# A planner's duration table for operations on few partitions, and the order of work at the beginning and at the entry of the MLP

## The chip, the cores and the metric

The kernel runs on one core of one Trainium2 chip. The metric is the device time of one execution in microseconds (us); the times of a kernel are told as the median of several executions. The engines are named as the profile names them: PE is TensorE's matmul, PEld its weight load, DVE is VectorE, ACT is ScalarE, POOL is GpSimd, SP is SyncE, whose queue issues most of the DMAs. [...]

## The reference

One layer of a decoder trunk in float32, with 1024 positions and a width of 1024, and 256 memory tokens:

```python
h = rms_norm(x, norm_mix)
p = h @ w_in                       # columns: RWKV r,k,v,w,a,g | conv B,C,x | gate A | gate B
p_rw = p_rw + (token_shift(p_rw) - p_rw) * mu_shift
out_a = rwkv7_branch(r, k, v, wd, ad, gd, ...)   # recurrence over 1024 positions, 8 heads of 64
out_b = short_conv_branch(cb, cc, cx, conv_w)    # B * conv3(C * x)
merged = sigmoid(ga + bg_a) * (out_a @ w_proj_a) + sigmoid(gb + bg_b) * (out_b @ w_proj_b)
x = x + merged @ w_out_mix
x = x + memory_cross_attention(rms_norm(x, norm_xattn), rms_norm(mem, norm_mem), ...)
hm = rms_norm(x, norm_mlp)
x = x + square(relu(hm @ w_up)) @ w_down         # 4096 hidden columns
return rms_norm(x, norm_final)
```

## The kernel before

All activations are held transposed: 128 columns of the width on the partitions, positions along the free axis, in two blocks of 512 positions. Every large matrix product is exact to float32 by splitting both factors into a high and a low part ("hi", "lo", type fp32r) and adding three matmuls of 128x128 by 128x512: hi by hi, hi by lo, lo by hi. A weight tile is loaded into a raw buffer (names `wr`), its hi half is made by ACT (`wh`) and its lo half by DVE (`wl`); a `+` behind such a name (`wr+`, `wh+`) marks a tile that lies in the large pool of 44 buffers called H, where the activations (`H`, `P`) live too.

**A planner sets the order.** The program is written as generators ("streams"): the main stream walks through the stages below, and side streams load weights, split them, make the constants, and do the recurrence. A `Scheduler` (lines 40 to 235) runs them in one pass when the program is built. Each instruction goes through `Proxy.call` (line 253, the line that nearly all rows of the profile show), which books it in `note` on a clock of its engine: it starts when its engine is free and its operands are written, and lasts what `cost` (line 68) says for ACT, DVE and POOL, and what `pe` (line 91) says for PE. `shared` (line 186) lengthens DVE's and POOL's operations on SBUF where they overlap. A stream that yields `need(tile)` (line 199) is called again once PE's planned clock has passed the planned end of the tile's writing by 0.7 us. So the table in `cost` does not change what is computed; it decides how many matmuls of the main stream are put on PE between two steps of a side stream, and which operation stands ahead of which on the in-order queues of DVE, ACT, POOL and SP. On the chip the engines wait for each other by semaphores; the planned clock is not there.

**The stages.** (1) The beginning: `x_stage` (line 997) transposes the two blocks of x on PE, each in two halves of four column groups; ACT and DVE take the transposes out of PSUM as hi and lo (`H`) with the gain applied, while the first pair of column tiles of the projection is accumulated in PSUM tiles psg and psy. `x_scale` (line 985) squares the block's rows on ACT, and gives the factor 1/rms, which PE transposes over the partitions (psg<-ident,sm) into `Rt`; the factor is applied when a tile is taken out. `constants` (line 686) transposes a table of gains (`vrow`, rows from DRAM in a tile st) on PE. (2) The projection, `gemm` over the list `PROJ` (line 584): 46 column tiles x 2 blocks, 24 matmuls for each block of a tile. `proj_evac` (line 1123) takes each out. Between these matmuls stand the steps of the recurrence as side streams: `wkv_prepares` (factors of a window of positions), `wkv_inverts` (products of 64x128 operands into pss, taken out by DVE on 64 partitions, and an inverse), `wkv_chains` (the state, 64x64 products in psc). There are eight windows. (3) `mem_k` and `mem_v` (lines 1623, 1640) make keys and values of the memory tokens with half-wide weights ("light" weights), then `merge` (line 1701) the two gated branches. (4) A residual product, the attention, a second residual product (h3). (5) The MLP: `up_products` (line 857) computes 16 pairs of tiles with seven products in place of eight (a Strassen-like scheme; `PRODUCTS`, line 842, gives for each its number p, PSUM tile, weight and half). A product is 4 operands k x 3 matmuls. Products 1 and 2 take the plain halves of the activations, products 6, 5, 7, 3 sums of them; `up_operands` (line 895) makes the sums on POOL and the hi and lo parts on ACT and DVE. The weights of a pair come as a "quad" of two raw buffers; `w_split_quad` (line 466) makes four weight tiles of it: the plain one (ACT, DVE), then four POOL operations, then three more. `w_splits` (line 509) does this quad after quad. (6) `mlp_down`, the same way.

The numbers behind a tile's name (psg_2075) count allocations. A tag has few buffers (3 of psg, 2 of pss, 2 of psc, 1 of psy; the raw buffers `wr` are 2 and some of H), so an instruction also waits for the reader of the buffer's last content.

Of the kernel before, what the change touches and what calls it, by code (L numbers as in the profile page):

```python
# [10 lines left out]
F32R = mybir.dt.float32r  # L11
# [30 lines left out]
class Scheduler:  # L42
# [25 lines left out]
    def cost(self, eng, meth, aps):  # L68
        n = self.size(aps[0])
        psum = any(self.key(a).startswith("ps") for a in aps)  # L70
        if eng == "ACT":
            return (0.05 if psum else 0.093) + (0.093 if len(aps) > 2 else 0.0) + n / 1200
        if eng == "DVE":
            if meth == "reciprocal":
                return 0.07 + n * 0.0066
            if meth == "tensor_reduce":
                n = self.size(aps[1])
# [181 lines left out]
def tile_hybrid_block(  # L259
# [147 lines left out]
    def w_raw(i):  # L407
        n = 2 if i in quads else 1
        more = i >= first_quad and (i - first_quad) % 2 if i in quads else i > first_quad and i % 4 > 1
# [15 lines left out]
    def w_loads():  # L425
        for i in range(2, len(wlist)):
            if i < first_quad:
                yield lambda: i < ws["split"] + 2
# [37 lines left out]
    def w_split_quad(raws):  # L466
# [15 lines left out]
        yield room_  # L482
        hi, lo = tiles()
        yield from halves(hi[:], lo[:], ra)
        w_made(hi, lo)
        yield need(lo)
# [22 lines left out]
    def w_splits():  # L509
        for i in range(2, len(wlist)):  # L510
            yield lambda: i < ws["raw"]
            raw = ws["raws"].pop(i)
            if i in quads:
                yield need(*raw) - 0.2
                yield from w_split_quad(raw)
                ws["split"] += 1
                ws["live"] -= 2
                continue
# [167 lines left out]
    def constants():  # L686
        yield until(("h", 0, 3))
        yield need(vrow) + 1.0
        vps = ps("y", [P, P])
# [167 lines left out]
    def up_products(ops, hook):  # L857
# [3 lines left out]
        for i in range(NP_):  # L861
            banks, wt, tmp = {}, [], {}
            if i == NP_ - 1:
                done.add(("up", "last"))
            for p, tag, w, half in PRODUCTS:
# [29 lines left out]
    def up_operands(raw, ops):  # L895


        t2 = {}
# [8 lines left out]

        yield until(("o", 1, 7))
        lh["n"] = 32
        for k in range(4):  # L910
# [4 lines left out]
            yield until(("h3", 0, 2 * k))  # L915
            a = raw[k][0]
            yield from make(1, k, a[:, 0], ("h3", 0, 2 * k))
            yield until(("h3", 0, 2 * k + 1))
            b = raw[k][1]
            yield from make(2, k, b[:, 0], ("h3", 0, 2 * k + 1))  # L920
            yield until(("h3", 1, 2 * k), ("h3", 1, 2 * k + 1))
# [63 lines left out]
    def x_scale(b, xs, ss):  # L985
        cs = slice(0 if b else TB, D)
        for i in range(4):
            ACT.activation(xs[i][:, cs], xs[i][:, cs], AF.Square, accum_out=ss[:, 4 + i:5 + i])
# [8 lines left out]
    def x_stage(b, tags):  # L997
# [7 lines left out]
        for h in range(2):  # L1005
# [8 lines left out]
            for k in range(4):  # L1014
# [11 lines left out]
                done.add(("h", b, n))  # L1026
        done.add(("x", b))
# [102 lines left out]
    def proj_stream(t, b, o):  # L1130
# [59 lines left out]
        elif kind == "cx":  # L1190
            if (i, b) == (3, 1):
                drop(1)
# [959 lines left out]
```

## Time and profile before

| | |
|---|---|
| time, median of 3 runs (lowest to highest) | 1808.51 us (1805.92 to 1813.68) |
| the profiled execution | 1810.48 us, of which its span 1808.8 us |
| mean granted clock of TensorE | 0.991 |
| busy: PE / PEld / DVE / ACT / POOL | 1745.7 / 1423.7 / 1078.6 / 696.6 / 524.4 us |
| moved by DMA | 289.19 MB |

The profile is one execution. A row of the timeline gives the start, the duration, the engine, the operation with out<-in, and how many like it follow one another; the bracket behind it holds the time the engine stood idle before it and what released it. A matmul's duration includes its passage through the array, and matmuls overlap: a 128x512 one reads 0.39 us, while the next one starts 0.23 us later. PE is busy for 97% of the span, so the views that matter are those of the other 63 us: what PE waited for, and where its clock was not granted in full.

### The profile page before, as it was taken

Reading aid. Unit: us, or ns where it says so; the run is one execution under the profiler, and the core shown is the slowest. Engines: PE = TensorE matmul, PEld = TensorE weight load, DVE = VectorE, ACT = ScalarE, POOL = GpSimd, SP = SyncE. Lnnn points to the kernel's source line nnn. Section 1 sums busy time; section 2 is a strip of 40 time slices with the busy share of each in tenths; the row PEclk is TensorE's granted clock in tenths of the full one; section 3 lists DMA queues with packets and bytes.
Section 4 is the critical chain, followed back from the end, with each engine's and each line's share of the span. In section 5 each row is a group of like instructions: output and inputs, shape, how many; then the busy total and the mean of one; then the engine's idle time right before and its main releaser. Section 6 shows DMA issues by size and latency. Waiting matters only on the chain.

```text
span 1808.8 us, 26674 instructions
## 1 busy us (share of the span) xinstructions
PE 1745.7 (97%) x9914; PEld 1423.7 (79%) x9914; DVE 1078.6 (60%) x1694; ACT 696.6 (39%) x1233; POOL 524.4 (29%) x872
## 2 busy tenths in 40 slices
PE   7899999999999999999999999999999999999998
PEld 5687777877767778988888877778888888888887
DVE  4478675665664443555546665577677776655543
ACT  4624333132234433422333334354444444534532
POOL 2117653664465110001323344342232310000000
PEclk9999999999999999999999999999999999999999
DMA  6543532423435436645745667334544469765431
GB/s 211 204 118 104 164 103 56 117 74 103 111 94 159 139 95 209 208 140 190 233 152 187 192 185 263 105 111 158 182 149 165 151 219 350 259 208 196 152 123 52
DMA packets 303360, 289.19 MB, mean 160 GB/s; under 512 B 40745, under 2 KB 223135, under 8 KB 303231
## 3 DMA queue, kind: packets, MB, share of 16 engines
q1 hardware_dynamic: 302158, 286.97, 49.7%
q8 instruction: 78, 1.28, 0.3%
q10 hardware_dynamic: 1072, 0.53, 0.1%
q14 instruction: 52, 0.42, 0.1%
HBM read 193.06 MB, written 94.37 MB: 159 GB/s over the span
## 4 chain that ended last, share of the span: by engine, by line
PE 75%; DVE 8%; DMA 5%; POOL 4%; issue 3%; ACT 3%; SPq 1%; ACTq 0%; POOLq 0%; DVEq 0%
PE psg L253 50%; PE pss L253 12%; PE psc L253 9%; DVE P L253 4%; PE psy L253 4%; POOL ex L253 3%; ACT P L253 2%; SPq L253 1%; DVE wl L253 1%; DMA sh<-d_ob 1%; DVE st L253 1%; POOL P L253 1%; DVE sh L253 1%; ACT st L253 1%; DMA P<-dn 1%
## 5 line engine op out<-in xcount | busy, mean ns | idle before, releaser
L253 PE MATMUL psg<-H,wh 128*128 128x512 f32 x1808 | 583.6, 400 | 2.6 <-ACT H L253 1.4
L253 PEld LDWEIGHTS psg<-H,wh 128*128 128x128 f32 x1808 | 338.1, 190 | 73.9 <-ACT H L253 2.3
L253 PE MATMUL psg<-P,wh 128*128 128x512 f32 (+1 forms) x1240 | 371.2, 380 | 6.6 <-ACT P L253 3.0
L253 PE MATMUL psg<-H,wl 128*128 128x512 f32 x888 | 355.2, 400 | 0.0
L253 PEld LDWEIGHTS psg<-P,wh 128*128 128x128 f32 x1240 | 227.9, 188 | 50.6 <-ACT P L253 3.4
L253 PE MATMUL psg<-P,wl 128*128 128x512 f32 (+1 forms) x620 | 235.6, 380 | 0.0
L253 ACT ACTIVATE wh<-wr 128x1024 fp32r<-128x1024 f32 (+2 forms) x187 | 137.8, 764 | 229.5 <-PE psg L253 126.2
L253 DVE TENSOR_TENSOR wl<-wr,wh 128x1024 fp32r<-128x1024 f32 (+2 forms) x178 | 161.2, 928 | 83.3 <-ACT wh L253 77.7
L253 PEld LDWEIGHTS psg<-H,wl 128*128 128x128 f32 x888 | 168.7, 190 | 34.3
L253 ACT ACTIVATE P<-P 128x512 fp32r<-128x512 f32 (+3 forms) x246 | 147.8, 635 | 78.5 <-DVE P L253 41.9
L253 DVE TENSOR_TENSOR P<-P,P 128x512 fp32r<-128x512 f32 (+2 forms) x204 | 150.2, 773 | 19.1 <-ACT P L253 17.8
L253 POOL TENSOR_TENSOR sm<-sm,mhalf 128x8 f32<-128x8 f32 (+2 forms) x18 | 23.7, 1317 | 427.6 <-DVE sm L253 427.6
L253 PEld LDWEIGHTS psg<-P,wl 128*128 128x128 f32 x620 | 116.8, 188 | 21.8 <-DVE wl L253 0.6
L253 POOL TENSOR_TENSOR ex<-ex,P 128x60 f32<-128x60 f32 (+24 forms) x248 | 97.4, 393 | 102.9 <-DMA P<-dn 88.1
L253 POOL TENSOR_TENSOR ex<-ex 128x60 f32<-128x60 f32 (+24 forms) x248 | 100.4, 405 | 19.4
L253 PE MATMUL pss<-P,wh 128*128 128x512 f32 x296 | 91.7, 390 | 1.1 <-DVE P L253 1.1
L253 ACT ACTIVATE P<-psc,sm 64x64 f32<-64x64 f32 (+1 forms) x128 | 42.4, 332 | 105.4 <-PE psc L253 62.3
L253 DVE TENSOR_SCALAR P<-psc,sm 64x64 f32<-64x64 f32 x120 | 34.9, 291 | 77.9 <-ACT P L253 72.6
L253 PE MATMUL psc<-P,P 128*64 128x64 f32 (+2 forms) x816 | 66.5, 247 | 12.9 <-DVE P L253 10.0
L253 DVE TENSOR_TENSOR P<-psg,P 128x512 f32<-128x512 f32 x44 | 30.3, 689 | 80.8 <-PE psg L253 67.5
L253 PEld LDWEIGHTS psc<-P,P 128*64 128x64 f32 (+2 forms) x816 | 45.2, 143 | 38.6 <-issue 17.2
L253 PE MATMUL psc<-P,wh 128*128 128x512 f32 x216 | 67.4, 393 | 0.0
(686 smaller groups left out, 2812.9 us busy)
## 6 DMA issues: line engine op xcount, KB each, us to landing
P<-d_t SPq DMA_DIRECT2D x56, 512.0 KB
wr<-in_w_in_dram SPq DMA_DIRECT2D x40, 512.0 KB
d_t<-P SPq DMA_DIRECT2D x64, 256.0 KB
d_x<-P SPq DMA_DIRECT2D x48, 256.0 KB
P<-d_x SPq DMA_DIRECT2D x24, 512.0 KB
d_t<-st SPq DMA_DIRECT2D x48, 256.0 KB
d_tg<-st SPq DMA_DIRECT2D x32, 256.0 KB
wr<-in_w_kv_dram SPq DMA_DIRECT2D x16, 512.0 KB
```

The source lines that it names most:

```text
L253: return fn(*args, **kw)
```

## The change

Seven edits, without a change to what is computed. (1) In `cost`, operations on fewer than 128 partitions get durations of their own: ACT 0.1 us more above 64 elements a partition; DVE 0.17 us (0.2 for scalar_tensor_tensor) with 0.08 more from 5 to 64 elements; and reciprocal and tensor_reduce on DVE get 0.11 and 0.12 us more. (2) The light weights use raw buffers in H as well, and after the projection are loaded up to four ahead; the tiles of `merge` are allocated one at a time. (3) Of the first two quads the plain weight tile is made first, of both, and then the rest of both. (4) `constants` waits 6 us rather than 1 us after the table's landing as planned, and transposes it in psg, not psy. (5) `up_products` takes products 1 and 2 of pairs 0 and 1, then the rest of pair 0, the rest of pair 1, and the others as before; the operands of products 1 and 2 are made by a stream of their own, ahead. (6) For the second block of x the squares are written to a spare tile and their stream is started between its two halves rather than after them. (7) Two waits keep the parts of a short-convolution tile in their order.

```diff
--- before.py
+++ after.py
@@ -67,14 +67,17 @@
         n = self.size(aps[0])
+        part = aps[0].shape[0] < 128
         psum = any(self.key(a).startswith("ps") for a in aps)
         if eng == "ACT":
-            return (0.05 if psum else 0.093) + (0.093 if len(aps) > 2 else 0.0) + n / 1200
+            return (0.05 if psum else 0.093) + (0.093 if len(aps) > 2 else 0.0) + n / 1200 + (0.1 if part and n > 64 else 0.0)
         if eng == "DVE":
             if meth == "reciprocal":
-                return 0.07 + n * 0.0066
+                return 0.18 + n * 0.0066
             if meth == "tensor_reduce":
-                n = self.size(aps[1])
+                return 0.19 + self.size(aps[1]) * 0.00104
+            if part:
+                return (0.2 if meth == "scalar_tensor_tensor" else 0.17) + (0.08 if 4 < n <= 64 else 0.0) + n * 0.00104
             if meth in ("tensor_scalar", "tensor_copy") and not psum:
@@ -406,7 +409,7 @@
         n = 2 if i in quads else 1
-        more = i >= first_quad and (i - first_quad) % 2 if i in quads else i > first_quad and i % 4 > 1
+        more = i >= first_quad and (i - first_quad) % 2 if i in quads else (i > first_quad or i in light) and i % 4 > 1
         raw = ws["raws"][i] = [sb("wr+" if more else "wr", wlist[i][1]) for _ in range(n)]
@@ -425,7 +428,7 @@
             if i < first_quad:
-                yield lambda: i < ws["split"] + 2
+                yield lambda: i < ws["split"] + (4 if i in light and "proj" in done else 2)
             else:
@@ -463,7 +466,7 @@
         ws["made"] += 1
-    def w_split_quad(raws):
+    def w_split_quad(raws, first=True, rest=True):
         n = KD // 2
@@ -479,11 +482,14 @@
         room_ = lambda: ws["made"] < ws["closed"] + 3
-        yield room_
-        hi, lo = tiles()
-        yield from halves(hi[:], lo[:], ra)
-        w_made(hi, lo)
-        yield need(lo)
+        if first:
+            yield room_
+            hi, lo = tiles()
+            yield from halves(hi[:], lo[:], ra)
+            w_made(hi, lo)
+        if not rest:
+            return
+        yield need(raws[0], raws[1])
         s2 = sb("st", [P, n, P])
@@ -511,10 +517,21 @@
                 yield need(*raw) - 0.2
-                yield from w_split_quad(raw)
-                ws["split"] += 1
-                ws["live"] -= 2
+                if i == first_quad:
+                    yield from w_split_quad(raw, rest=False)
+                    before = raw
+                elif i == first_quad + 1:
+                    yield from w_split_quad(raw, rest=False)
+                    for r in (before, raw):
+                        yield from w_split_quad(r, first=False)
+                        ws["split"] += 1
+                        ws["live"] -= 2
+                else:
+                    yield from w_split_quad(raw)
+                    ws["split"] += 1
+                    ws["live"] -= 2
                 continue
@@ -685,8 +702,8 @@
         yield until(("h", 0, 3))
-        yield need(vrow) + 1.0
-        vps = ps("y", [P, P])
+        yield need(vrow) + 6.0
+        vps = ps("g", [P, P])
         yield need(vps)
@@ -858,11 +875,14 @@
-        for i in range(NP_):
-            banks, wt, tmp = {}, [], {}
+        all_ = [({}, [], {}) for _ in range(NP_)]
+        order = [(i, PRODUCTS[:2]) for i in range(2)] + [(i, PRODUCTS[2:]) for i in range(2)] + \
+            [(i, PRODUCTS) for i in range(2, NP_)]
+        for i, products in order:
+            banks, wt, tmp = all_[i]
             if i == NP_ - 1:
                 done.add(("up", "last"))
-            for p, tag, w, half in PRODUCTS:
+            for p, tag, w, half in products:
                 if w == len(wt):
@@ -895,6 +915,7 @@
@@ -905,20 +926,22 @@
             done.add(("up", p, k))
+        def plain():
+            for k in range(4):
+                for e in range(2):
+                    yield until(("h3", 0, 2 * k + e))
+                    yield from make(1 + e, k, raw[k][e][:, 0])
         lh["n"] = 32
+        sch.spawn(plain(), first=True)
         for k in range(4):
             t2[k] = tt[:, k % 2]
-            yield until(("h3", 0, 2 * k))
-            a = raw[k][0]
-            yield from make(1, k, a[:, 0], ("h3", 0, 2 * k))
-            yield until(("h3", 0, 2 * k + 1))
-            b = raw[k][1]
-            yield from make(2, k, b[:, 0], ("h3", 0, 2 * k + 1))
-            yield until(("h3", 1, 2 * k), ("h3", 1, 2 * k + 1))
+            yield until(("up", 1, k), ("up", 2, k), ("h3", 1, 2 * k), ("h3", 1, 2 * k + 1))
+            a, b = raw[k]
             yield need(a, b)
@@ -984,8 +1007,9 @@
         cs = slice(0 if b else TB, D)
+        junk = sb("P", [P, D]) if b else None
         for i in range(4):
-            ACT.activation(xs[i][:, cs], xs[i][:, cs], AF.Square, accum_out=ss[:, 4 + i:5 + i])
+            ACT.activation(junk[:] if b else xs[i][:, cs], xs[i][:, cs], AF.Square, accum_out=ss[:, 4 + i:5 + i])
         yield need(ss)
@@ -1024,8 +1048,9 @@
                 done.add(("h", b, n))
+            if h == (1, 0)[b]:
+                sch.spawn(x_scale(b, xs, ss))
         done.add(("x", b))
-        sch.spawn(x_scale(b, xs, ss))
         for k in range(KD):
@@ -1190,6 +1215,7 @@
                 drop(1)
+            yield until(("cc", i, b))
             u = sb("sh", [P, TB + 2])
@@ -1209,7 +1235,9 @@
             prevs["cy", i, b] = y
+            done.add(("cy", i, b))
         elif kind == "cb":
+            yield until(("cy", i, b))
             z = sb("st", [P, TB])
@@ -1702,6 +1730,8 @@
         wh, wl = w_[0]
+        for t in (mgh, mgl):
+            t.append(two(sb("H", [P, S], F32R)))
         for b in range(NB):
@@ -2094,8 +2124,7 @@
         done.add("proj")
-        mgh = [two(sb("H", [P, S], F32R)) for _ in range(KD)]
-        mgl = [two(sb("H", [P, S], F32R)) for _ in range(KD)]
+        mgh, mgl = [], []
         for k, n in MIX:
```

Edits (1) and (6) move other work than their own lines. On ACT at the beginning, before (P_98 to P_104 are the rows of the second block, H_164 to H_167 the hi parts of its second half's columns, st_482 an operand of the decay's small product):

```order
L253 ACTIVATE P_184<-psg_390 128x512
L253 ACTIVATE H_164<-pss_398,gmix 128x512
L253 ACTIVATE st_482<-sh_445,omu 128x512
L253 ACTIVATE st_487<-sh_448,omu 128x512
L253 ACTIVATE H_165<-pss_399,gmix 128x512
L253 ACTIVATE P_181<-pss_399 128x512
L253 ACTIVATE H_166<-psc_400,gmix 128x512
L253 ACTIVATE H_167<-psc_401,gmix 128x512
L253 ACTIVATE P_183<-psc_401 128x512
L253 ACTIVATE P_98,sm_194<-P_98 128x1024
...
L253 ACTIVATE P_104,sm_194<-P_104 128x1024
L253 ACTIVATE st_482<-st_482 64x512
```

and in the change:

```order
L256 ACTIVATE P_179<-psc_313 128x512
L256 ACTIVATE P_453,sm_194<-P_98 128x1024
...
L256 ACTIVATE P_453,sm_194<-P_104 128x1024
L256 ACTIVATE st_478<-sh_434,omu 128x512
L256 ACTIVATE st_483<-sh_437,omu 128x512
L256 ACTIVATE H_164<-pss_445,gmix 128x512
L256 ACTIVATE H_165<-pss_446,gmix 128x512
L256 ACTIVATE P_181<-pss_446 128x512
L256 ACTIVATE H_166<-psc_447,gmix 128x512
L256 ACTIVATE P_183<-psc_448 128x512
L256 ACTIVATE P_524<-st_478 64x512 x4
```

The four squares stand ahead of the second half's hi parts instead of behind them, and the small product's operand (P_524<-st_478) follows those hi parts at once.

On PE in the third window of the recurrence (pss_2102<-cmat is the running sum of the window's decays, pss_2126<-P,P the first product that needs its result; psg_2075 is a column tile of the projection), before:

```order
L253 MATMUL pss_2102<-cmat,P_1721 128x128 x4
L253 MATMUL psg_2075<-H_163,wl_1914 128x512
L253 MATMUL psg_2075<-H_164,wh_1913 128x512
L253 MATMUL psg_2075<-H_172,wh_1913 128x512
L253 MATMUL psg_2075<-H_164,wl_1914 128x512
L253 MATMUL psg_2075<-H_165,wh_1913 128x512
L253 MATMUL pss_2126<-P_1878,P_1880 128x128
```

and in the change:

```order
L256 MATMUL pss_2131<-cmat,P_1812 128x128 x4
L256 MATMUL psg_2110<-H_170,wh_1997 128x512
L256 MATMUL psg_2110<-H_162,wl_1998 128x512
L256 MATMUL psg_2110<-H_163,wh_1997 128x512
L256 MATMUL psg_2110<-H_171,wh_1997 128x512
L256 MATMUL psg_2110<-H_163,wl_1998 128x512
...
L256 MATMUL psg_2110<-H_164,wl_1998 128x512
L256 MATMUL psg_2110<-H_165,wh_1997 128x512
L256 MATMUL psg_2110<-H_173,wh_1997 128x512
L256 MATMUL psg_2110<-H_165,wl_1998 128x512
L256 MATMUL pss_2165<-P_1911,P_1913 128x128
```

Five matmuls of the projection stood between the sum and the product that needs it; now there are eleven. In the order of the eight windows, this distance was 12, 15, 5, 4, 15, 3, 11 and 6, and is 6, 31, 11, 6, 6, 4, 6 and 9. The next distance, to the second group of such products, was 20, 17, 20, 13, 20, 13, 20 and 10, and is 30, 19, 25, 16, 31, 19, 25 and 20.

On PE at the entry of the MLP (psg_10918 was pair 0's product 6, with the sums' operands; psc_10935 its product 2), before:

```order
L253 MATMUL psc_10935<-P_10904,wh_10754 128x512 x2
L253 MATMUL psc_10935<-P_10904,wl_10755 128x512
L253 MATMUL psg_10918<-P_10444,wh+_1494_10822 128x512 x2
L253 MATMUL psg_10918<-P_10444,wl+_1495_10823 128x512
L253 MATMUL psg_10918<-P_10619,wh+_1494_10822 128x512 x2
L253 MATMUL psg_10918<-P_10619,wl+_1495_10823 128x512
```

and in the change:

```order
L256 MATMUL psc_10928<-P_10865,wh_10752 128x512 x2
L256 MATMUL psc_10928<-P_10865,wl_10753 128x512
L256 MATMUL psg_10967<-P_10356,wh+_1493_10815 128x512 x2
L256 MATMUL psg_10967<-P_10356,wl+_1494_10816 128x512
...
L256 MATMUL psc_10983<-P_10865,wh+_1493_10815 128x512 x2
L256 MATMUL psc_10983<-P_10865,wl+_1494_10816 128x512
L256 MATMUL psg_10910<-P_10450,wh_10902 128x512 x2
L256 MATMUL psg_10910<-P_10450,wl_10903 128x512
```

Behind pair 0's product 2 stand 24 matmuls of pair 1 (psg_10967, psc_10983), with plain operands that pair 0 has used, and only then pair 0's product 6.

## The prediction, as put on record

> **What bounds the kernel now.** I read the page's busy times and chain first, then PE's waits, then these by stage.
>
> ```profile
> PE 1745.7 (97%) x9914; PEld 1423.7 (79%) x9914; DVE 1078.6 (60%) x1694; ACT 696.6 (39%) x1233; POOL 524.4 (29%) x872
> PE 75%; DVE 8%; DMA 5%; POOL 4%; issue 3%; ACT 3%; SPq 1%; ACTq 0%; POOLq 0%; DVEq 0%
> ```
>
> PE is busy for 1745.7 of 1808.8 us and holds 75% of the chain that ended last. The change takes no matmul away, so it can only win from the 63 us in which PE stood idle, and from stretches in which its clock was low. PE's longest waits over the whole span:
>
> ```profile
> PE pss L253 <- DVE P L253: 15.0, 16, 2.1
> PE psc L253 <- DVE P L253: 11.0, 10, 4.5
> PE psy L253 <- DMA st<-in_norm_final_dram: 3.8, 1, 3.8
> PE psc L253 <- DVE sh L253: 3.4, 7, 1.5
> PE psg L253 <- ACT wh L253: 1.4, 1, 1.4
> ```
>
> The columns are the total in us, the number of waits and the longest. The last row is from the same view of 700 to 780 us, the rest of the whole span. By stage (start:end, length, then busy us and count of PE, PEld, DVE, ACT and POOL, then the granted clock):
>
> ```profile
> 100.00:600.00 500.00, 477.88 (x3631) 376.00 (x3630) 325.40 (x591) 158.18 (x308) 271.91 (x647) 0.99 0.38 108
> 1168.00:1201.00 33.00, 25.49 (x110) 19.09 (x110) 27.19 (x33) 18.18 (x33) 18.40 (x13) 0.95 0.15 48
> ```
>
> So 22.1 us are idle in the projection with the recurrence, 7.5 at the MLP's entry, and the two longest single waits, 4.5 and 3.8 us, are at the beginning. The rest is in smaller pieces, most of them there, in the attention and at the end.
>
> **The beginning.** On PE (first three rows and the matmuls behind) and on DVE (fourth):
>
> ```profile
> 24.20 0.45 PE L253 MATMUL psy<-ident,st 128*128 128x128 f32 x1 [3.77 <-DMA st<-in_norm_final_dram]
> 37.82 1.04 PE L253 MATMUL psc<-ident,P 128*128 128x128 f32 x2 [1.01 <-DVE P L253]
> 56.70 0.76 PE L253 MATMUL psc<-P,P 128*128 128x512 f32 x1 [4.46 <-DVE P L253]
> 24.68 0.29 DVE L253 COPY vec<-psy 128x128 f32<-128x128 f32 x1 [2.15 <-PE psy L253]
> 58.54 1.05 PE L253 MATMUL psg<-H,wh+_62_343 128*128 128x512 f32 x2
> 59.39 0.63 PE L253 MATMUL psg<-H,wl+_63_344 128*128 128x512 f32 x1
> 65.22 0.62 PE L253 MATMUL psg<-H,wh+_62_343 128*128 128x512 f32 x2
> 65.68 0.39 PE L253 MATMUL psg<-H,wl+_63_344 128*128 128x512 f32 x1
> ```
>
> Edit (4) takes the transposition of the gains out from under the DMA: 3.77 us of PE idle go. But PE is soon held again by DVE, which empties the transposes of x (37.82, 1.01 us), and DVE itself was held for only 2.15 us behind that table's copy. So of the 3.77 the path keeps at most 2.15; I take 2.0, and the second half of the block comes 2.0 us earlier. The cover of the transposition's new place is the pair's own matmuls.
>
> Edit (6) is about the 4.46 us. There PE waits for the operands of the decay's small product, and these stood behind the squares on ACT:
>
> ```profile
> 47.77 1.09 ACT L253 ACTIVATE P<-P 128x1024 f32<-128x1024 f32 x1
> 50.90 1.08 ACT L253 ACTIVATE P<-P 128x1024 f32<-128x1024 f32 x1
> 51.94 0.64 ACT L253 ACTIVATE st<-st 64x512 f32<-64x512 f32 x1
> 52.60 3.23 ACT L253 ACTIVATE P<-st 64x512 fp32r<-64x512 f32 x5
> 43.30 0.69 ACT L253 ACTIVATE H<-pss,gmix 128x512 fp32r<-128x512 f32 x1 [5.73 <-PE pss L253]
> ```
>
> Four squares take from 47.77 to 51.94, 4.2 us. In the change they run in the 5.73 us in which ACT waited for the second half's transposes (last row); that idle time is their cover. Without it the second half's hi parts, and PE's matmuls on them, come up to 4.2 us late. The small product is also planned behind the first matmuls of the next tile. So the wait of 4.46 goes, and the slow clock behind it: a hi pair took 0.85 us from 58.54 to 59.39, against 0.46 from 65.22 to 65.68, so 0.2 us a matmul, and over six of them, which I take for the slow stretch, 1.2. [...] **Sum: 2.0 + 4.46 + 1.2 = 7.7 us**, from 3.5 (the squares' 4.2 us not covered) to 11 (all of 3.77 kept, and its own slow matmuls).
>
> **The projection and the recurrence.** PE's waits from 100 to 660 us, then three windows on PE, the third's copies on DVE, then DVE's small operations and its evacuations by form (count, total and mean ns of one, idle before):
>
> ```profile
> PE pss L253 <- DVE P L253: 13.3, 13, 2.1
> PE psc L253 <- DVE P L253: 5.6, 8, 1.1
> 171.55 1.13 PE L253 MATMUL pss<-P,P 64*128 64x128 f32 x14 [2.06 <-DVE P L253]
> 225.45 1.13 PE L253 MATMUL pss<-P,P 64*128 64x128 f32 x14 [1.01 <-DVE P L253]
> 531.97 1.13 PE L253 MATMUL pss<-P,P 64*128 64x128 f32 x14 [1.47 <-DVE P L253]
> 223.58 1.73 DVE L253 COPY P<-pss 64x256 f32<-64x256 f32 x4
> L253 DVE COPY P<-pss 64x256 f32<-64x256 f32 x32 | 13.5, 422 | 0.6
> L253 DVE TENSOR_SCALAR P<-psc,sm 64x64 f32<-64x64 f32 x120 | 34.9, 291 | 77.9 <-ACT P L253 72.6 <-POOL ex L253 4.4
> L253 DVE TENSOR_TENSOR st<-psg,P 128x512 f32<-128x512 f32 x32 | 22.1, 690 | 25.7 <-PE psg L253 25.4
> L253 DVE TENSOR_TENSOR sh<-psg,P 128x512 f32<-128x512 f32 x19 | 13.1, 690 | 14.7 <-PE psg L253 14.5
> ```
>
> Each of the eight windows has one wait like that at 225.45, where PE's first group of 64x128 products comes before the four copies out of pss are done: window 2 lost 2.06, window 3 1.01, the last 1.47 us, and the eight together 10.0 of the 13.3. The old table gives a copy of 64x256 0.07 + 256 x 0.00104 = 0.336 us, the new one 0.436; measured are 0.422. For a 64x64 step of the chain it gave 0.137, now 0.317; measured are 0.291. So the old plan was 0.35 us short on the four copies and 0.31 on each pair of chain steps, and the new one is not short. In window 3, six more matmuls of 0.23 us stand before the group: 1.4 us against a wait of 1.01. But three windows get shorter distances (12, 15 and 11 become 6), with nothing between DVE's sum and copies there now; that holds only as far as the plan does. I leave 3 of the 10.0 us: 7.0 won. The chain's eight waits shrink by 0.31 each, 2.5; other waits on pss by 0.5. **Sum: 10.0 us.** Above, the bound is 13.3 + 5.6 = 18.9; below, -4.5, if no wait goes and the three shorter distances cost their 20 matmuls of 0.23 us. The chain's last step comes 110 matmuls of the main stream later (25 us), but 267 of them (61 us) still follow before the merging.
>
> **Keys and values.** The wait of 1.4 us for `wh` is for a weight still on its way; edit (2) loads it earlier, past SP's other issues of that stretch. **1.4**, from 0.
>
> **The attention.** 3.4 us in seven waits. Ahead of each the plan is now longer by 0.11 (reciprocal) and 0.12 (reduce): 0.23 x 7 = **1.6**, from -1 (edits elsewhere move DVE's queue) to 3.4.
>
> **The MLP's entry.** PE's waits from 1159 to 1202 us, the first of them, and DVE's and POOL's operations there beside the same one later (the x92 row is 1201 to 1700):
>
> ```profile
> PE psg L253 <- DVE P L253: 3.4, 4, 1.1
> PE psg L253 <- ACT P L253: 3.0, 1, 3.0
> PE pss L253 <- DVE P L253: 1.1, 2, 0.7
> 1173.26 0.50 PE L253 MATMUL psg<-P,wh 128*128 128x512 f32 x1 [3.00 <-ACT P L253]
> 1192.64 7.46 DVE L253 TENSOR_TENSOR P<-P,P 128x512 fp32r<-128x512 f32 x6
> L253 DVE TENSOR_TENSOR P<-P,P 128x512 fp32r<-128x512 f32 x92 | 60.6, 708 | 13.6 <-ACT P L253 13.3
> 1159.60 1.29 POOL L253 TENSOR_TENSOR wr<-wr,wr 128x512 f32<-128x512 f32 x1 [23.87 <-DVE wl L253]
> 1196.63 1.73 POOL L253 TENSOR_TENSOR wr+_1488_10757<-wr+_1488_10757,st 128x512 f32<-128x512 f32 x1
> ```
>
> The first wait (3.00) is for product 1's last operand, which comes from the last tile of the residual product; it is behind the same work as before and stays. The first of DVE's waits, 0.78 us, is for the lo part of that operand and stays too. What edit (5) covers is the rest: 3.4 + 1.1 - 0.78 = 3.7 us of waits for the sums' lo parts. The 24 matmuls of pair 1 ahead of them last 24 x 0.23 = 5.5 us, so they cover these 3.7. They take the cover from later, too: DVE is busy for 27.19 of 33.0 us in this stretch, gets two more half-tiles of weight there, and is slowed by POOL, since its operation takes 7.46 / 6 = 1.24 us here against 0.71 later. I take 0.7 off: **3.0 us**. Bounds: 7.5 of idle and about 1.4 of slow clock behind it make 8.9; if the two half-tiles come ahead of the operands, at 1.24 each, -2.5.
>
> [...]
>
> **Sum against the profiled execution:** 7.7 + 10.0 + 1.4 + 1.6 + 3.0 = 23.7, and 1810.5 - 23.7 = 1786.8: **1787 us**. That execution is 0.1% above the median of the runs, 1808.5, which I leave inside the range.
>
> **Rivals.** (a) *The interleaved pairs feed PE fully*: the operand of 1173.26 comes early as well, and the entry wins 8.9 instead of 3.0: 1781. For it: the stream of plain operands is put ahead of all others. Against: DVE's 27.19 of 33. (b) *The recurrence's waits only move*: the gain there is 0, since DVE also waits for POOL and ACT, which the plan knows no better than before: 1797. For it: window 2 waited longest (2.06 us) with a distance of 15 matmuls, the last 1.47 with 6, window 3 1.01 with 5, so distance is not all. (c) *The change does not do what it says*: the squares aren't covered (3.5) and (b) holds, the rest brings 4: 1803. Against: ACT's 5.73 us idle stands right there. (d) *Slower*: with longer small operations in the plan, DVE gets them ahead of the evacuations of psg, and PE waits for a bank. The two largest forms alone are 32 + 19 = 51 evacuations. This decides from 23.7 / 51 = 0.46 us of wait at each; at 0.69 us, one operation as long as an evacuation ahead of every one, it costs 35 and gives 1822. Against: DVE waits 25.4 and 14.5 us for psg in these rows, so evacuations come early now.
>
> **Chances.** The forecast's own case (1778 to 1794) 0.53, (a) 0.14, (b) 0.19, (c) 0.09, (d) 0.05. About 0.5%, 9 us, is what a measurement of this kernel tells from no change. The forecast, (a) and (b) are faster by more: 0.86; (c) is the same: 0.09; (d) slower: 0.05. The range takes in (a) and (b) and ends before (c): **1772 to 1800**; below 1778 the terms would have to go near their upper bounds together.
>
> **What would show it.** No wait of 3.8 us for the norm table's DMA and none of 4.5 us for the decay's operands, and the tile behind the pair starting near 50.8 instead of 58.54. In 100 to 660, PE's waits on DVE under 10 us instead of 18.9; those of the first groups near zero in windows 2 and 3 if the table is the cause. At the MLP, the wait near 3.0 us still there and none for the sums' lo parts. The prediction is wrong if 100 to 600 keeps 22 us of idle, or if PE waits for banks of psg there.

## The result, and the profile after

| | |
|---|---|
| the changed kernel, median of 6 runs (lowest to highest) | 1796.54 us (1794.25 to 1803.41) |
| the kernel before, beside it | 1807.12 us (1805.68 to 1813.68, 6 runs) |
| ratio, 95% interval | 0.9943 (0.9919 to 0.9968) |
| the same, measured again with 6 runs | 0.9955 (0.9938 to 0.9973) |

The change saves 8 to 10 us, 0.45 to 0.57%. The forecast was 23.7 us, to 1787 us. The direction was right, and less than half of the sum arrived: the time lies in the range that was given, but outside the forecast's own case (1778 to 1794). The first profile of the changed kernel is of its slowest run (1803.41 us, span 1801.7); a second one was taken of a run with a span of 1797.7 us, and where it matters the text says which of the two a row is from.

The page's busy times, PE's longest waits over the span, its waits from 100 to 660 us, and two stages, all of the first profile after:

```profile
PE 1745.5 (97%) x9914; PEld 1423.6 (79%) x9914; DVE 1081.4 (60%) x1694; ACT 698.2 (39%) x1233; POOL 519.6 (29%) x872
```

```profile
PE pss L256 <- DVE P L256: 8.3, 10, 1.9
PE psc L256 <- ACT st L256: 7.9, 5, 3.7
PE pss L256 <- ACT P L256: 5.0, 5, 3.0
PE pss L256 <- issue: 2.9, 3, 2.0
PE psc L256 <- DVE P L256: 2.8, 3, 1.7
```

```profile
PE pss L256 <- DVE P L256: 5.5, 8, 1.7
PE pss L256 <- ACT P L256: 5.0, 5, 3.0
PE pss L256 <- issue: 2.2, 2, 2.0
PE psc L256 <- ACT st L256: 1.7, 1, 1.7
PE pss L256 <- POOL sh L256: 1.4, 1, 1.4
PE psc L256 <- DVE P L256: 1.1, 2, 0.7
```

```profile
100.00:600.00 500.00, 486.50 (x3673) 384.59 (x3672) 321.81 (x585) 154.01 (x298) 263.32 (x644) 0.99 0.38 108
600.00:700.00 100.00, 96.31 (x774) 73.19 (x773) 37.99 (x81) 40.09 (x85) 12.49 (x13) 0.98 0.40 124
```

PE's busy time is what it was (1745.7; in the second profiles 1743.0 before and 1743.0 after), so the saving is idle time. Slow clock was not saved over the whole span: the mean granted clock was 0.991 and 0.993 in the two profiles of the kernel before, and is 0.989 in both after. The waits on DVE are the ones that fell: on pss from 15.0 to 8.3 us, on psc from 11.0 to 2.8; from 100 to 660 us from 18.9 to 6.6. What is new stands in the other rows: 7.9 us on ACT's `st` (2.7 before), 5.0 on ACT's `P` (1.6 before), 2.9 with no releaser that the profile shows ("issue", 0.8 before), 1.4 on POOL. The idle time of 100 to 600 us fell from 22.1 to 13.5 us, and from 600 to 700 us 3.7 us came up, where the kernel before had 0.2 (PE 99.83 of 100 there): 5.1 us less over both. In the second profiles of the two kernels it is 1.9 less (20.0 before, 18.1 after).

### The profile page after: what moved, and what is told of

It reads as the page before. It is cut to its first block, busy times and chain, and to the rows that moved or that the text cites. A ratio compares the mean times of both kernels' runs of the same rounds, so it can differ in the third digit from the quotient of the medians.

```text
span 1801.7 us, 26657 instructions
## 1 busy us (share of the span) xinstructions
PE 1745.5 (97%) x9914; PEld 1423.6 (79%) x9914; DVE 1081.4 (60%) x1694; ACT 698.2 (39%) x1233; POOL 519.6 (29%) x872
## 5 line engine op out<-in xcount | busy, mean ns | idle before, releaser
L256 ACT ACTIVATE wh<-wr 128x1024 fp32r<-128x1024 f32 (+2 forms) x155 | 127.1, 839 | 209.4 <-PE psg L256 143.1
L256 DVE TENSOR_TENSOR wl<-wr,wh 128x1024 fp32r<-128x1024 f32 (+2 forms) x146 | 149.6, 1040 | 62.0 <-ACT wh L256 61.1
L256 POOL TENSOR_TENSOR ex<-ex 128x60 f32<-128x60 f32 (+24 forms) x248 | 95.7, 386 | 19.4
L256 PEld LDWEIGHTS psc<-P,P 128*64 128x64 f32 (+2 forms) x816 | 44.8, 141 | 34.5 <-issue 11.6
```

The costliest lines, as they stand in the source:

```text
L256: return fn(*args, **kw)
```

## The experiments

First each part alone, put on the kernel before; then the two places at which the trace after shows new waits. A table of all timed runs, with the saving against the kernel before worked out as (1 - ratio) x 1807 us:

| kernel | ratio (95% interval) | saves, us |
|---|---|---|
| the change, first and second time | 0.9943 (0.9919 to 0.9968), 0.9955 (0.9938 to 0.9973) | 10.3, 8.1 |
| duration table alone | 0.9978 (0.9967 to 0.9989) | 4.0 |
| beginning alone | 0.9988 (0.9978 to 0.9998) | 2.2 |
| MLP's entry alone | 0.9993 (0.9981 to 1.0005) | 1.3 |
| light weights alone, first and second time | 0.9961 (0.9948 to 0.9975), 0.9983 (0.9970 to 0.9996) | 7.0, 3.1 |
| kernel before, small products' results out of the staging tiles | 0.9974 (0.9963 to 0.9985) | 4.7 |
| the change, small products' results out of the staging tiles | 0.9912 (0.9897 to 0.9926) | 15.9 |
| the same without the change of the beginning | 0.9949 (0.9935 to 0.9962) | 9.2 |
| the change, memory tokens planned later | 0.9957 (0.9942 to 0.9972) | 7.8 |
| the change, second quad's sums on POOL later | 0.9952 (0.9933 to 0.9971) | 8.7 |

The four parts alone add up to 10.6 us with the second timing of the light weights, 14.5 with the first; the whole saves 8 to 10.

### The duration table alone

The edit is the one of `cost`, with the two waits for the short convolution:

```diff
+        part = aps[0].shape[0] < 128
...
+            if part:
+                return (0.2 if meth == "scalar_tensor_tensor" else 0.17) + (0.08 if 4 < n <= 64 else 0.0) + n * 0.00104
```

> Only the duration table of the planner is changed (with the two waits that keep a short-convolution tile's parts in order). Theory A, the forecast's: it is worth 10.0 + 1.6 us, so about 1796 us against 1807 of the kernel before, and PE's waits on DVE from 100 to 660 us fall from 18.9 to under 10. Theory B, from the changed kernel's trace: the waits on DVE shrink but others (on ACT, on SP's queue) come in their place, so about half of it is left: 1801 to 1804 us.

Measured: a ratio of 0.9978, 4.0 us (2.0 to 6.0), which is theory B's size or a little less. The stage of 100 to 600 us in this kernel:

```profile
100.00:600.00 500.00, 484.80 (x3676) 383.18 (x3674) 323.47 (x585) 158.99 (x305) 263.94 (x649) 1.00 0.38 111
```

Idle fell from 22.1 to 15.2 us: 6.9 won. But PE's waits from 690 to 760 us, among the keys and values, rose from 1.4 us to 5.8:

```profile
PE psg L256 <- ACT wh L256: 3.8, 4, 2.2
PE psg L256 <- DVE wl L256: 2.0, 1, 2.0
```

PE reaches that stage at 694.2 us instead of 704.8, its weights do not come as much sooner, and 4.4 of the 6.9 us are lost there, in a place that the table does not speak of. In the whole change the light weights' edit stands against this loss: from the first key tile to the merging it takes 48.0 and 48.2 us in its two profiles, and 54.7 with the table alone.

### The beginning alone

The gains' transposition 6 us after its planned landing and into psg, and the second block's squares between its halves:

```diff
-        yield need(vrow) + 1.0
-        vps = ps("y", [P, P])
+        yield need(vrow) + 6.0
+        vps = ps("g", [P, P])
...
+            if h == (1, 0)[b]:
+                sch.spawn(x_scale(b, xs, ss))
```

> Only the beginning is changed: the later transposition of the gains, and the squares of the second block between its halves. Theory A: 7.7 us less, about 1799 us. Theory B: the projection's first tile starts 6 to 7 us earlier, but by 100 us PE stands where it stood before, since the staging tiles of the decay's and the rate's small products are freed by transfers that end no earlier: 1805 to 1808 us, with a wait of PE on ACT's st of 3 us or more between 60 and 90 us.

Measured: 2.2 us (0.4 to 4.0), theory B. The wait of 4.46 us is gone from its trace, and in its place stand four waits on ACT's `st` between 50 and 100 us, 5.5 us in all, where the first profile of the kernel before had two, of 2.0. The mechanism is best read in the first profile of the whole change, on PE (two rows), ACT (two rows), DVE and SP's queue (two rows):

```profile
51.97 0.61 PE L256 MATMUL psg<-H,wh+_62_342 128*128 128x512 f32 x2
...
79.64 1.22 PE L256 MATMUL psc<-P,P 128*128 128x512 f32 x2 [3.73 <-ACT st L256]
...
70.94 1.27 ACT L256 ACTIVATE st<-psc,hw 128x512 f32<-128x512 f32 x2 [1.39 <-PE psc L256]
...
78.90 1.30 ACT L256 ACTIVATE st<-psc,ha 128x512 f32<-128x512 f32 x2 [5.22 <-DMA d_sw<-st]
...
72.56 1.22 DVE L256 TENSOR_TENSOR wl<-wr,wh 128x1024 fp32r<-128x1024 f32 x1
...
73.85 0.38 SPq L256 DMA_DIRECT2D wr<-in_w_in_dram  x1
74.28 0.57 SPq L256 DMA_DIRECT2D d_sw<-st  x1
```

The next tile starts at 51.97 instead of 58.54, 6.6 us earlier. That is no chance of one execution: it starts at 54.6 to 59.4 us in the eight profiles of this study without the new beginning, 57.7 in the mean, and at 49.9 to 52.0 in the six with it, 51.1 in the mean. The forecast named 50.8, 7.7 earlier, but the 1.2 us of slow clock in it lie behind this tile's start; the two waits ahead of it, 2.0 + 4.46, make 6.5 and arrived. By 100 us they are gone again: in the first 100 us PE is busy for 80.8 and 81.8 us in the two profiles of the kernel before, and for 80.8 and 81.8 in the two of the change. The results of the small products (16 tiles of 128x512 for the decay and the rate) go out through the four staging tiles `st`. At 78.90 ACT gets a staging tile back that it has waited 5.22 us for. Its transfer was issued at 74.28, behind a weight load on SP's queue, which was issued at 73.85, right after DVE's last read of that buffer (72.56 + 1.22). The data of that transfer came from the first ACT operation at 70.94, so they stood ready for more than 2 us before the issue, and ACT went on 4.6 us behind it: more of the delay is the transfer itself than its place in the queue. So the earlier start ran into transfers that did not come earlier, and the slow clock moved along: it is 0.50 from 79.6 to 83.0 us, where the first profile of the kernel before has 0.50 from 58.5 to 61.5, and the pair of matmuls at 79.64 takes 1.22 us, against 0.61 at 51.97, where the clock is 1.00. That the weight load held the queue is read from these times; it was not tried apart from the staging tiles.

### Light weights alone, twice

```diff
-                yield lambda: i < ws["split"] + 2
+                yield lambda: i < ws["split"] + (4 if i in light and "proj" in done else 2)
```

with the second pair of raw buffers in the large pool, and the merging's tiles one at a time.

> Only the weights of keys and values are loaded further ahead, with the merging's tiles allocated one at a time. Theory A: 1.4 us less, about 1806 us. Theory B: nothing, 1807 us, since the weight's low part then waits on DVE.

Measured: 7.0 us (4.5 to 9.4), more than either theory allowed. The order of this kernel is that of the kernel before up to some 650 us, but its profile stands 3.6 us ahead at 100 us. So it was run again.

> The early light weights alone, a second time. The first measurement gave 7.0 us, while its trace has 3.1 us between the first key tile and the merging, and the program up to 650 us is that of the kernel before. If 7.0 is right: 1800 to 1801 us again. If the trace is right: 1803 to 1805 us.

Measured the second time: 3.1 us (0.7 to 5.4). Both traces need 46.1 us from the first key tile to the merging, where the two profiles of the kernel before need 49.2 and 49.4. 3.1 us is what the traces support; the first number, from 6 runs, is not explained by anything in its trace, and executions of one program differ by as much (below). The two intervals have 4.5 to 5.4 us in common, so a gain a little above 3.1 is not ruled out. Of the 3.1 us, the 1.4 of the forecast is the wait that a view shows; the rest is closer spacing of the matmuls (PE was busy for 47.83 us in this stage before, and for 46.10 here, at a clock of 1.00 in both), which no row of the waits names.

### The MLP's entry alone

The reordered products with their operands, and the plain tiles of both quads first (the diff's parts on `up_products`, `up_operands`, `w_split_quad` and `w_splits`).

> Only the entry of the MLP is changed: both first quads' plain tiles first, products 1 and 2 of two pairs first, their operands in a stream of their own. Both theories: 2 to 3 us less, 1804 to 1805 us; the rival that feeds PE fully: 8.9 us less, 1798 us.

Measured: 1.3 us (-0.9 to 3.4), unclear by itself. The traces tell it apart. From the start of the first product's first matmul to the end of the 168th (14 products of 12), the seven profiles with the order before read 52.0 to 53.6 us, and the seven with the new order 49.2 to 51.2: the means are 1.9 us apart, and the two groups don't overlap.

### Second profiles of both kernels

> The kernel before, profiled a second time. If the first profile was an ordinary execution, its wait for the norm table's DMA (3.8 us, with slow matmuls behind it) is there again and the first light weight is used near 704.8 us. If that wait was longer than usual (another kernel with the same program up to 650 us showed 2.3 us and no slow matmuls, and stood 3.6 us earlier at 100 us), it is shorter here and the point near 701 us.

Measured: 1804.96 us, one run. It stands at the keys at 699.8 us, 5.0 us before the first profile. The wait for the norm table's DMA was 3.5 us, neither as long as the first nor as short as in the light weights' kernel. The point that settles what this wait is worth is the same program in two kernels whose order there is that of the kernel before. Light weights alone, PE and then 20 to 35 us:

```profile
22.64 0.30 PE L253 MATMUL psy<-ident,st 128*128 128x128 f32 x1 [2.25 <-DVE P L253]
```

```profile
20.00:35.00 15.00, 10.88 (x56) 8.09 (x54) 11.23 (x19) 10.66 (x22) 6.32 (x23) 1.00 0.84 269
```

The MLP's entry alone, the same two views:

```profile
24.39 0.45 PE L253 MATMUL psy<-ident,st 128*128 128x128 f32 x1 [5.09 <-DMA st<-in_norm_final_dram]
```

```profile
20.00:35.00 15.00, 10.61 (x47) 8.70 (x48) 6.82 (x12) 6.33 (x14) 4.48 (x18) 0.77 0.74 245
```

From one execution to another the wait ahead of this matmul ran from 2.25 to 5.09 us, and the clock of 20 to 35 us from 1.00 to 0.77 (at 2.25 the last releaser was DVE, and no longer the DMA). One profile's 3.77 was a draw from that. Edit (4) takes away a wait of varying size: it is there in each of the eight profiles with the transposition in its old place, of which seven read a clock of 0.77 to 0.89, and in none of the six with the new one, which read 0.95 to 1.00.

> The changed kernel, profiled a second time, and timed in more runs. The first profile was of its slowest execution (1803.4 us against a median of 1796.5). If that is chance at the beginning, this profile reaches the keys and values 3 to 6 us earlier than 699.8 us, and waits for ACT's st near 80 us less than the 3.7 us of the first. If not, the same waits are there. Median 1796 to 1798 us.

Measured: 1798.28 us (1793.36 to 1801.47), and the keys at 698.4 us, 1.4 earlier than in the first profile and not 3 to 6. The wait on ACT's `st` near 80 us is there again, 3.59 us. So it belongs to the kernel and is no chance of the slowest run.

### The small products' results out of the staging tiles

```diff
-            z = sb("st", [P, TB])
+            z = sb("P", [P, TB]) if dst is not d_g else sb("st", [P, TB])
             fin(z, o2, j)
```

This was put on the changed kernel, on the kernel before, and on the changed kernel with the beginning as before.

> The changed kernel, with the results of the decay's and the rate's small products kept in tiles of the large pool in place of the four staging tiles st, so that ACT need not wait there for a transfer out of a staging tile. Theory B (the gain at the beginning is given back to those staging tiles): PE's waits on ACT's st from 55 to 90 us, 6.2 us in the first profile, fall under 2 us, and the time by 3 to 5 us, to about 1792 us. Theory A' (the beginning's gain arrives at the end of the projection as it is): no change, 1796 us.

> The kernel before, with the results of the decay's and the rate's small products in tiles of the large pool, and nothing of the change. If the staging tiles were the place to which the beginning's gain went (Theory B), they cost little here, since PE waits only 1.6 to 1.8 us for them before: 1804 to 1805 us against 1806. If they cost time by themselves, whatever the beginning looks like, this wins 6 to 7 us as it did in the changed kernel: 1799 to 1800 us.

> The changed kernel with the small products' results in the large pool, but without the change of the beginning (squares behind both halves, early transposition of the gains, as before). With the beginning it took 1790.8 us, a ratio of 0.9912. Theory B (the beginning's gain is real and was lost at the staging tiles): without it 5 to 7 us are missing, ratio 0.994 to 0.995. Theory C (the staging tiles cost 5 to 6 us by themselves, whatever the beginning looks like, as the kernel before with them alone suggests with 4.7): ratio 0.992 to 0.9925, and the beginning is worth 2 us or less.

Measured: 1790.75 us (0.9912) on the changed kernel; 1801.13 (0.9974) on the kernel before; 1799.10 (0.9949) on the changed kernel without its beginning. The stretch from 50 to 100 us (PE's busy time first, the clock in the third column from the end) in the second profile of the kernel before, the second of the change, the change with the results out of the staging tiles, and that without the beginning (a profile of the slowest of its five runs):

```profile
50.00:100.00 50.00, 44.49 (x183) 35.82 (x184) 26.03 (x41) 27.80 (x43) 7.55 (x19) 0.93 0.55 186
```

```profile
50.00:100.00 50.00, 44.39 (x179) 35.15 (x179) 24.57 (x39) 25.09 (x39) 5.19 (x11) 0.93 0.62 206
```

```profile
50.00:100.00 50.00, 49.71 (x222) 40.33 (x220) 31.88 (x52) 26.56 (x41) 6.76 (x14) 1.00 0.67 226
```

```profile
50.00:100.00 50.00, 46.21 (x193) 37.37 (x193) 26.14 (x44) 30.84 (x50) 7.94 (x19) 0.93 0.62 211
```

With the change alone, PE does no more in this stretch than before: 44.39 against 44.49 us, both at 0.93. With the results out of the staging tiles it does 49.71 at a clock of 1.00. Without the beginning it is back at 46.21 and 0.93. The difference in time between the last two kernels, (0.9949 - 0.9912) x 1807 = 6.7 us, is what the beginning is worth once the staging tiles are out of its way (by the two intervals, 3 to 10): close to the 7.7 forecast, within theory B's 5 to 7 and above theory C's 2. The kernel before's own gain from this edit, 4.7 us, is larger than theory B expected (1 to 2). So part of the 5.6 to 7.8 us that the edit wins in the changed kernel is its own, and the two shares were not told apart to better than a few us.

The changed kernel with this edit is the fastest of the study, 15.9 us (13.4 to 18.6) below the kernel before.

### The memory tokens' normalization planned later

In the second profile of the change, PE near 604 us, ACT, and SP's queue:

```profile
604.61 0.48 PE L256 MATMUL pss<-ident,P 128*128 128x128 f32 x1 [3.46 <-ACT P L256]
...
599.48 1.06 ACT L256 ACTIVATE P<-P 128x1024 f32<-128x1024 f32 x1 [4.16 <-DMA P<-in_mem_dram]
...
594.18 0.38 SPq L256 DMA_DIRECT2D wr<-in_w_in_dram  x1
594.61 1.05 SPq L256 DMA_DIRECT2D P<-in_mem_dram  x2
```

and SP's queue in the second profile of the kernel before:

```profile
575.40 0.92 SPq L253 DMA_DIRECT2D P<-in_mem_dram  x2
580.60 0.38 SPq L253 DMA_DIRECT2D wr<-in_w_in_dram  x1
```

The memory tokens' load now stands behind a weight load, where it stood ahead of one, so it is issued 0.4 us behind that instead of 5.2 us ahead. PE waits 3.46 us for its transposes. The edit gives the plan more distance:

```diff
-            yield need(mt[m])
+            yield need(mt[m]) + 6.0
             ACT.activation(junk[:], mt[m][:], AF.Square, accum_out=ss[:, m:m + 1])
```

> The changed kernel, with 6 us more of planned distance between the memory tokens' landing and their normalization. Theory B (the weight load ahead of that transfer on SP's queue waits for its buffer, so the transfer starts late): the wait of 3.5 us for ACT near 604 us goes, and the kernel takes 3 to 4 us less, 1793 to 1794 us. If that wait is only the place where another delay shows, PE waits as long elsewhere before the keys: 1797 us.

Measured: 1797.66 us, ratio 0.9957; no gain over the change that can be told. The wait at 604 us is gone, and PE's waits from 570 to 760 us are others, 6.6 us where the change had 6.5:

```profile
PE psg L256 <- DVE wl L256: 2.8, 2, 2.6
PE psc L256 <- DVE P L256: 2.3, 1, 2.3
PE pss L256 <- issue: 1.5, 1, 1.5
```

So theory B's mechanism is in the rows and its price is not: the projection's end is held by several chains of about the same length, and taking one away shows the next. That is read from two single profiles, and the one of this run is of its fastest execution (1790.43 us).

### The second quad's sums on POOL later

In the second profile of the change the MLP's entry has five waits, 1.72, 0.40, 0.73, 0.73 and 0.84 us, all on DVE's `P`. The last four come 1.7 us apart, which is DVE's pace there: four splits in 6.86 us while POOL ends the second quad's sums and then makes two operand sums.

```profile
1178.96 6.86 DVE L256 TENSOR_TENSOR P<-P,P 128x512 fp32r<-128x512 f32 x4
...
1180.14 1.74 POOL L256 TENSOR_TENSOR wr+_1488_10755<-wr+_1488_10755,st 128x512 f32<-128x512 f32 x1
```

The edit:

```diff
                     for r in (before, raw):
+                        if r is raw:
+                            yield until(("up", 7, 3))
                         yield from w_split_quad(r, first=False)
```

> The changed kernel, with POOL's four sums of the second quad held until the operands of product 7 are split; PE's order is unchanged. If POOL slows DVE there, the four waits of 0.4 to 0.8 us at the MLP's entry (2.7 us) go, the low parts of product 7 take 0.7 us each in place of 1.7, and the kernel takes 2 to 3 us less, 1794 to 1795 us. If the waits come from POOL's operand sums or from ACT, they stay: 1797 us. If pair 1 then waits for its weights, a new wait of PE on wh or wl shows behind 1200 us.

Measured: 1798.39 us, ratio 0.9952; no gain that can be told. Five waits of 0.64 to 0.77 us and two of 0.24 took the place of the four. The rows of this kernel say why, DVE and then POOL:

```profile
1175.56 2.48 DVE L256 TENSOR_TENSOR P<-P,P 128x512 fp32r<-128x512 f32 x4
1181.14 6.79 DVE L256 TENSOR_TENSOR P<-P,P 128x512 fp32r<-128x512 f32 x5 [3.10 <-ACT P L256]
...
1174.89 5.55 POOL L256 TENSOR_TENSOR P<-P,P 128x512 f32<-128x512 f32 x2
1180.40 1.29 POOL L256 TENSOR_TENSOR wr+_1488_10755<-wr+_1488_10755,wr+_1489_10756 128x512 f32<-128x512 f32 x1
1181.77 1.61 POOL L256 TENSOR_TENSOR st<-wr+_1489_10756,wr+_1488_10755 128x512 f32<-128x512 f32 x1
```

The condition is met when the operands are planned, not when they are split, so only two of POOL's operand sums moved ahead of the quad's, and the quad's sums still fall on the next five splits (6.79 us, 1.36 each). In the first row DVE kept its pace (0.62 us a split) while POOL's two sums took 5.55 us instead of 2 x 1.29; in the second POOL nearly kept its pace (1.29 and 1.61 us a sum) and DVE lost. So the edit moved the loss from one engine to the other and did not remove it. DVE and POOL still ran beside each other here, so what the entry would win without POOL stays open.

## Why the prediction was right in direction and too large

**The bound.** Right in that PE's busy time is unchanged and what was saved is idle time. The slow clock that the sum also counted did not show as a saving over the whole span (0.991 and 0.993 before, 0.989 after).

**The number.** 1797 us is what rival (b) gave, and that is luck: (b) took the recurrence's gain away and kept all the rest, while in the runs the recurrence and its surroundings kept a part, and it was the beginning that gave its gain back. The sum was also counted from one execution, of 1810.5 us; from the kernel's median of 1807 it would have named 1783.

**The beginning, 7.7 us forecast, 2.2 (0.4 to 4.0) measured.** The two edits did what the prediction said: the gains' wait and the 4.46 us are gone, and the next tile starts 6.6 us earlier. The failed step is its sum, which stopped at that tile. It priced ACT's squares and their cover, and did not ask which buffers the earlier results go into. These are the staging tiles, freed by transfers on SP's queue, and the gain was given back there by 100 us. With them out of the way the beginning is worth 6.7 us. The 2.0 us taken for edit (4) were not measured apart from edit (6).

**The recurrence, 10.0 forecast; the table as a whole 11.6 with the attention, 4.0 (2.0 to 6.0) measured.** The waits on DVE fell by 12.3 of 18.9 us, more than the 10.0 forecast, but distance explains that only in part. The eight windows' first groups waited for 10.0 us before and 5.2 in the first profile after. The third window, with 11 matmuls in place of 5, no longer waits; but the fifth and the seventh, whose distances fell to 6, stand idle for no more than 0.1 us either, while the fourth, with 6 in place of 4, waits 1.68 us after 1.54. Which part of the fall is distance and which is the changed order on DVE's queue was not told apart. What failed is the step from waits to time. Waits on ACT, POOL, the staging tiles and PE's issue came in their place (3.1 us before, 10.3 after, in 100 to 660 us, so 7.2 of the 12.3 came back), and a changed order moved the memory tokens' load behind a weight load. From 100 to 700 us PE's idle time fell by 5.1 us in the first profiles and by 1.9 in the second. That is rival (b) in part, which had been given 0.19. The window with a distance of 31 matmuls, the longest, still waits in both profiles of the change, now for POOL's `sh` (1.9 us in the second): more distance did not help there, since the releaser is no longer DVE.

**Keys and values, 1.4 forecast, 3.1 measured alone (trace and second timing).** Right in mechanism, too small for the edit alone, because the term was the one wait that the view shows, and the matmuls of the stage moved closer together besides. In the whole change the stage went from 49.2 and 49.4 us to 48.0 and 48.2, so 1.2 us: the forecast's size, but because a wait on DVE's `wl` came up there (1.3 and 1.8 us).

**The attention, 1.6 forecast.** From the merging's start to the first product of the MLP the seven profiles with the old table read 410.9 to 414.1 us, 411.9 in the mean, and the seven with the new one 411.1 to 413.4, 412.1 in the mean: nothing of this term shows. PE's waits on DVE's `sh` fell from 3.4 us to 1.5, while two on psy (1.2 and 2.4 us) stand there, where the kernel before had one of 0.6, and one of 1.1 on psg.

**The MLP's entry, 3.0 forecast, 1.3 (-0.9 to 3.4) measured, 1.9 in the traces.** The size was within its bounds, and the steps behind it were wrong. The prediction kept the 3.00 and 0.78 us and struck out the five waits behind them. The trace shows the reverse: product 1's waits and the 1.14 us are gone, a wait of 1.72 us came for product 2, and the four for the last sums' low parts stayed (2.7 us). The stream of plain operands did come early, as rival (a) said, and DVE beside POOL is the pace of the rest: in the first profile 1.72 us a split from 1182.66 on, while POOL works, and 0.62 us from 1193.06 on, while it stands idle. The 24 matmuls of cover (5.5 us) were set against waits that came one after another at DVE's pace, and by the order of the rows pair 1's first products had used up that cover before them.

**Rival (d)** did not happen: no wait of PE for an evacuation of psg shows in the projection.

## What to carry to other kernels

When a wait is removed near the start of a stage, follow the saved time to the next buffer that is recycled by a transfer, and to the place of that transfer in its queue. Here the same edit was worth 2 us in a kernel with the results in four staging tiles, and 6.7 in one with them in the large pool. Sum up the waits by what releases them: a planner that is corrected for one engine's durations clears that engine's waits and uncovers the others'. And profile the same program twice before pricing a wait for a DMA, since what read 3.8 us in one execution was anything from 2.3 to 5.1 in others.

## What the runs showed of the hardware that was not expected

A short idle time can be followed by a slow clock. In the second profile of the change, 180 to 183 and 183 to 187.4 us:

```profile
180.00:183.00 3.00, 1.19 (x17) 0.97 (x16) 2.90 (x6) 0.56 (x1) 0.00 (x0) 1.00 0.52 162
183.00:187.40 4.40, 4.31 (x12) 3.03 (x12) 1.78 (x4) 1.24 (x3) 0.00 (x0) 0.61 1.05 351
```

PE stood idle for 1.90 us there, behind sixteen 64-row matmuls, and the clock was 0.61 in the next 4.4 us. The kernel before has such places too. In the recurrence's second window, in its second profile:

```profile
168.83 1.88 PE L253 MATMUL pss<-P,P 64*128 64x128 f32 x14 [2.08 <-DVE P L253]
```

The clock was 0.57 in the 4 us from 168.8. In the first profile of the same kernel the same products, behind 2.06 us of idle, took 1.13 us (the row at 171.55 in the prediction), at a clock of 1.00. So it does not go by the length of the wait alone, and it differs from one execution to another; what decides it, and whether the small matmuls ahead of the wait have a part in it, was not tried. Waits of the recurrence can cost slow clock besides (0.61 over 4.4 us and 0.57 over 4 us in these two places), which the forecast's sum does not have. The other surprise is how far executions of one program lie apart without any change: the MLP's entry alone and the light weights alone have the same order until some 650 us, and reach the keys at 704.4 and 698.4 us. Of these 6.0 us, 3.3 are idle time and 2.8 are PE's busy time for the same matmuls (661.4 and 658.6 us, at a mean clock of 0.98 and 0.99).
